# Second FFN of a decoder layer: gate and up products side by side, two of eight row-block pairs by Strassen's seven products, and middle activations turned through a scratch in device memory

## The chip, the cores and the metric

One core of a Trainium2 chip runs the whole kernel. The metric is device time in microseconds (us) of one execution. The kernel before takes 2143.4 us, the median of three runs (2143.32 to 2143.5).

## What is computed

A decoder layer of model width 2048 on 16 learned positions and 256 tokens, in float32. It has a first FFN, a mixing part (sparse attention and a gated convolution, merged and projected by `W_out`) and a second FFN. The change is in the second FFN and the few steps ahead of it:

```python
u = rms_norm(h, ffn2_norm_g[l])
h = h + 0.5 * swiglu(u, ffn2_w_gate[l], ffn2_w_up[l], ffn2_w_down[l])
...
def swiglu(x, w_gate, w_up, w_down):
    return (jax.nn.silu(x @ w_gate) * (x @ w_up)) @ w_down
```

`w_gate` and `w_up` are 2048 x 5632, `w_down` is 5632 x 2048. Only the 256 tokens go through the second FFN.

## The kernel before

Every number is held as two parts, a high one (rounded to the form that TensorE multiplies, float32r) and a low one (what is left). A product is three matmuls: high x high, high x low, low x high.

**The stream.** All weights come in one fixed order through the class `Stream`. A *load* is 1 MB, 128 partitions x 2048 columns, by a DMA from the SP queue (L100) into one of three buffers `raw`. A load is cut into *pieces* of 1024 columns. `split` (L106 to L122) turns a piece into `whi` by ScalarE (L115, a copy with rounding) and `wlo` by VectorE (L116, a difference); there are four buffers of each. `next()` (L137 to L147) gives TensorE the next piece: it first has the piece three ahead split, then runs what is due, and then hands over the piece. So the program order of ScalarE and VectorE is: split of piece n + 3, the work due at step n, split of piece n + 4, and so on. A later load is issued on SP when the last piece of the load three before it has been split.

**Work due.** `later(fn, lag)` puts `fn` behind the split of the step that is `lag - 1` ahead. All of VectorE's and ScalarE's work in the second FFN besides splits is ordered by these lags alone.

**The second FFN** (`ffn_tokens`, L487 to L541) goes through 5632 middle columns in 11 *blocks* of 512, in two groups of 6 and 5. In a block the 256 tokens are two tiles of 128 (j = 1, 2). The activations `act` are stationary, the weights move, 512 columns at a time. Gate first: 16 row blocks of 128 (k), in 8 pieces of two, 12 matmuls a piece (2 tiles x 2 row blocks x 3), into two PSUM banks `pg`. Then up in the same way into `pu`. `gate` (L505) is Silu on ScalarE, `times` (L509) multiplies on VectorE into `s`. As the down products need the middle activations with the middle columns on partitions, `turn_columns` turns `s` into `mt` by 16 transposes of VectorE on 32 partitions each, and `split_into` (L339) makes the two parts in `mid`. After a group's blocks the down products run over `mid`, 512 output columns at a time, and are added to the residual `ht`.

**Ahead of it** the products with `W_out` run in four groups g of 512 columns. `add_out` adds them to `ht` (L1047) and squares on ScalarE; `turn_columns` turns `ht`, and `to_act` (ScalarE L1061, VectorE L1062) makes the activations of row blocks 4g to 4g + 3. For g = 3 the turning runs two quarters a step, inside the first block of the second FFN.

PSUM has eight banks: a ring of four single ones (`mm_tile`) and one of two doubles (`aux_tile`).

Of the kernel before, what the change touches and what calls it, by code (L numbers as in the profile page):

```python
# [9 lines left out]
F32 = mybir.dt.float32  # L10
F32R = mybir.dt.float32r
# [4 lines left out]
P = 128  # L16
# [46 lines left out]
LATER = LINE - META  # L63
SUB = 1024
RAW = 2048


class Stream:
# [7 lines left out]
    def __init__(self, nc, raw_pool, split_pool):  # L76
        self.nc, self.raw_pool, self.split_pool = nc, raw_pool, split_pool
        self.loads, self.subs = [], []
        self.raw, self.ready = {}, {}
        self.n_loaded = self.n_split = self.at = 0  # L80
        self.blocks, self.waiting, self.steps = [], [], []
        self.first = []

    def add(self, src, n, width, cuts=()):
# [21 lines left out]
    def split(self, upto):  # L106
        nc = self.nc
        while self.n_split < min(upto, len(self.subs)):
            g, c, kk, width = self.subs[self.n_split]
            self.load(g + RAW_BUFS)  # L110
            n = kk * width
            raw = self.raw[g][:, c : c + n]
            hi = self.split_pool.tile([P, SUB], F32R, name="whi")
            lo = self.split_pool.tile([P, SUB], F32R, name="wlo")
            nc.scalar.activation(hi[:, :n], raw, AF.Copy)  # L115
            nc.vector.tensor_sub(lo[:, :n], raw, hi[:, :n].bitcast(F32))  # L116
# [45 lines left out]
def tile_decoder_layer(  # L162
# [51 lines left out]
    for n in GROUPS:  # L214
        chunks(wgu2, gu, gu + 8 * n, 512)
        chunks(wd2, down, down + 4 * n, 512)
        gu, down = gu + 8 * n, down + 4 * n
# [90 lines left out]
    def tokens(ps_of, x, n):  # L308

        k = 0  # L310
        while k < n:
            blocks = [st.next()] + st.rest()
            for j, ps in ps_of.items():
                for i, (whi, wlo) in enumerate(blocks):
# [3 lines left out]
                    nc.tensor.matmul(ps, xlo, whi, start=False, stop=k + i == n - 1)  # L318
            k += len(blocks)

    def act_tokens(k, j, part):
# [165 lines left out]
    def ffn_tokens():  # L487

        with tc.tile_pool(name="ffn2", bufs=1, reuse_waits="tile") as fp:
            mid = fp.tile([P, 4 * GROUPS[0], 2, SEQ], F32R, name="mid")  # L490

            late["junk"] = lambda: fp.tile([P, 512], F32, name="junk")
            late["mt"] = lambda: fp.tile([P, 4, SEQ], F32, name="mt", bufs=2)
# [6 lines left out]

            st.later(add_up, 4)
            st.later(root, 5)
            st.later(inverse, 6)

            def gate(pg, s):  # L505
                for j in (1, 2):
                    nc.scalar.activation(s[:, j - 1], pg[j], AF.Silu, scale=rcol[:, 0, j - 1 : j])

            def times(pu, s):  # L509
                for j in (1, 2):  # L510
                    nc.vector.scalar_tensor_tensor(
                        s[:, j - 1], pu[j], rcol[:, 0, j - 1 : j], s[:, j - 1], op0=ALU.mult, op1=ALU.mult
                    )

            def add(d, j, pd, last):
# [6 lines left out]
            for c, n in enumerate(GROUPS):  # L522
                for f in range(n):
                    s = fp.tile([P, 2, 512], F32, name="s", bufs=2)
                    mt = fp.tile([P, 4, SEQ], F32, name="mt", bufs=2)
                    pg = {j: mm_tile(f"pg{j}") for j in (1, 2)}
                    tokens(pg, act_tokens, KD)
                    st.later(lambda pg=pg, s=s: gate(pg, s))
                    pu = {j: mm_tile(f"pu{j}") for j in (1, 2)}
                    tokens(pu, act_tokens, KD)  # L530
                    st.later(lambda pu=pu, s=s: times(pu, s))
# [32 lines left out]
    with ExitStack() as mix:  # L564
# [501 lines left out]
        for g in range(4):  # L1066
# [78 lines left out]
def _layout(x, meta_tokens, ffn1_norm_g, ffn1_w_gate, ffn1_w_up, ffn1_w_down, mix_norm_g, w_in, q_norm_g,  # L1145
# [31 lines left out]
    a["wo"] = _chunks(_tiles(w_out[0], 512))  # L1177
    gu = np.stack([_tiles(ffn2_w_gate[0], 512), _tiles(ffn2_w_up[0], 512)], 1)
    a["wgu2"] = _chunks(gu.reshape(-1, P, KD * 512))
    a["wd2"] = _down_columns(ffn2_w_down[0])  # L1180
# [20 lines left out]
```

## Time and profile before

| what | us |
|---|---|
| median of three runs | 2143.4 |
| span of the profiled execution (first to last instruction) | 2141.4 |
| second FFN, from its first weight load into TensorE to the span's end | 722.6 |
| TensorE busy | 2136.3 |
| TensorE's weight loads busy | 1921.2 |
| VectorE busy | 1325.8 |
| ScalarE busy | 954.5 |

The profiled execution's own time is its span and what lies around it; the median of the runs is 2.0 us above this span. PE is TensorE, PEld its loading of stationary data, DVE is VectorE, ACT is ScalarE, SP the engine whose queue issues the transfers. Lines of groups read: line, engine, operation, tile written <- tiles read, shape, count | busy us, mean ns of one | idle us before it, and what ended most of it. The lines of stretches read: stretch, its length, busy us of PE, PEld, DVE, ACT and POOL with the number of instructions in brackets, granted clock of TensorE, share of DMA time, GB/s. Matmuls are pipelined and their recorded durations overlap.

### The profile page before, as it was taken

To read this page: it belongs to the slowest core of one execution; us is meant where nothing else is said; L and a number is where in the kernel's file an instruction comes from. 1 tells how busy PE (TensorE), PEld (TensorE's weight loads), DVE (VectorE), ACT (ScalarE), POOL (GpSimd) and SP (SyncE) were. 2 spreads that over 40 slices of the span, in tenths; PEclk is the share of its full clock that TensorE was granted. 3 is DMA by queue.
4 is the path that set the end of the run, shared out by engine and by line. 5 is a ranking of instruction groups with operands and counts; after the bars stand their busy time and mean duration, and the time that the engine had idled before them with its cause. 6 is when DMAs were issued, how large, how long until landed. Compare 5 with 4: busy or idle time off the path is not lost.

```text
span 2141.4 us, 30929 instructions
## 1 busy us (share of the span) xinstructions
PE 2136.3 (100%) x12902; PEld 1921.2 (90%) x12902; DVE 1325.8 (62%) x1776; ACT 954.5 (45%) x1173; POOL 10.0 (0%) x28
## 2 busy tenths in 40 slices
PE   9999999999999999999999999999999999999999
PEld 9999999999999998799988888888888888888887
DVE  7555544455555556677686487886676644666664
ACT  6444433344444445565444444454444433444442
POOL 0000000000000000000000000000000000000000
PEclk9999999999999999999999999999999999999999
DMA  7555545555544545454555555555555555555554
GB/s 267 189 181 179 179 180 178 178 177 177 177 178 178 177 170 177 159 176 158 172 188 194 194 189 204 177 183 210 196 196 186 196 191 195 196 197 195 189 200 143
DMA packets 56909, 397.58 MB, mean 186 GB/s; under 512 B 6337, under 2 KB 7105, under 8 KB 9409
## 3 DMA queue, kind: packets, MB, share of 16 engines
q1 hardware_dynamic: 55872, 393.51, 53.4%
q8 instruction: 101, 1.65, 0.3%
q10 hardware_dynamic: 576, 1.05, 0.1%
q0 software_dynamic: 320, 1.05, 0.1%
q14 instruction: 40, 0.32, 0.0%
HBM read 393.49 MB, written 2.10 MB: 185 GB/s over the span
## 4 chain that ended last, share of the span: by engine, by line
PE 99%; DMA 0%; DVE 0%; SPq 0%; ACT 0%; issue 0%; ACTq 0%
PE pd L290 4%; PE pd L289 4%; PE pd L288 4%; PE pu L289 4%; PE pg L289 4%; PE pg L288 4%; PE pu L288 4%; PE pu L290 4%; PE pg L290 4%; PE pg L317 4%; PE pg L318 4%; PE pd L318 4%; PE pu L317 4%; PE pg L316 4%; PE pu L316 4%; PE pd L316 4%
## 5 line engine op out<-in xcount | busy, mean ns | idle before, releaser
L116 DVE TENSOR_TENSOR wlo<-raw,whi 128x1024 fp32r<-128x1024 f32 (+1 forms) x749 | 912.7, 1220 | 780.6 <-ACT whi L115 777.6
L115 ACT ACTIVATE whi<-raw 128x1024 fp32r<-128x1024 f32 (+1 forms) x749 | 788.3, 1055 | 1079.2 <-PE pd L289 146.3
L288 PE MATMUL pd<-mid,whi 128*128 128x272 f32 x704 | 201.7, 286 | 0.0
L289 PE MATMUL pd<-mid,whi 128*128 128x272 f32 x704 | 201.7, 286 | 0.0
L290 PE MATMUL pd<-mid,wlo 128*128 128x272 f32 x704 | 201.7, 286 | 0.0
L288 PE MATMUL pu<-act,whi 128*128 128x272 f32 x672 | 192.6, 287 | 0.0
L289 PE MATMUL pu<-act,whi 128*128 128x272 f32 x672 | 192.5, 287 | 0.0
L288 PE MATMUL pg<-act,whi 128*128 128x272 f32 x672 | 192.5, 286 | 0.0
L289 PE MATMUL pg<-act,whi 128*128 128x272 f32 x672 | 192.5, 286 | 0.0
L290 PE MATMUL pg<-act,wlo 128*128 128x272 f32 x672 | 192.5, 286 | 0.0
L290 PE MATMUL pu<-act,wlo 128*128 128x272 f32 x672 | 192.5, 286 | 0.0
L317 PE MATMUL pg<-wlo,act 128*128 128x512 f32 x352 | 137.2, 390 | 0.0
L318 PE MATMUL pg<-whi,act 128*128 128x512 f32 x352 | 137.1, 389 | 0.0
L316 PE MATMUL pg<-whi,act 128*128 128x512 f32 x352 | 136.9, 389 | 0.0
L316 PE MATMUL pu<-whi,act 128*128 128x512 f32 x352 | 136.9, 389 | 0.0
L317 PE MATMUL pu<-wlo,act 128*128 128x512 f32 x352 | 136.9, 389 | 0.0
L318 PE MATMUL pu<-whi,act 128*128 128x512 f32 x352 | 136.9, 389 | 0.0
L316 PE MATMUL pd<-whi,mid 128*128 128x512 f32 x352 | 136.9, 389 | 0.0
L317 PE MATMUL pd<-wlo,mid 128*128 128x512 f32 x352 | 136.9, 389 | 0.0
L318 PE MATMUL pd<-whi,mid 128*128 128x512 f32 x352 | 136.9, 389 | 0.0
L288 PEld LDWEIGHTS pd<-mid,whi 128*128 128x128 f32 x704 | 132.6, 188 | 0.0
L289 PEld LDWEIGHTS pd<-mid,whi 128*128 128x128 f32 x704 | 132.6, 188 | 0.0
(248 smaller groups left out, 4014.3 us busy)
## 6 DMA issues: line engine op xcount, KB each, us to landing
raw<-in_wgu_dram SPq DMA_DIRECT2D x174, 1024.0 KB, 4.8
raw<-in_wd_dram SPq DMA_DIRECT2D x88, 1024.0 KB, 4.8
raw<-in_wcv_dram SPq DMA_DIRECT2D x24, 1024.0 KB, 4.8
raw<-in_wgc_dram SPq DMA_DIRECT2D x24, 1024.0 KB, 4.9
raw<-in_wga_dram SPq DMA_DIRECT2D x24, 1024.0 KB, 4.8
raw<-in_wo_dram SPq DMA_DIRECT2D x16, 1024.0 KB, 4.8
raw<-in_wqi_dram SPq DMA_DIRECT2D x8, 1024.0 KB, 4.9
raw<-in_wq_dram SPq DMA_DIRECT2D x8, 1024.0 KB, 4.8
```

The costliest lines, as they stand in the source:

```text
L115: nc.scalar.activation(hi[:, :n], raw, AF.Copy)
L116: nc.vector.tensor_sub(lo[:, :n], raw, hi[:, :n].bitcast(F32))
L288: nc.tensor.matmul(ps, whi, xhi, start=first, stop=False)
L289: nc.tensor.matmul(ps, whi, xlo, start=False, stop=False)
L290: nc.tensor.matmul(ps, wlo, xhi, start=False, stop=last)
L316: nc.tensor.matmul(ps, xhi, whi, start=k + i == 0, stop=False)
L317: nc.tensor.matmul(ps, xhi, wlo, start=False, stop=False)
L318: nc.tensor.matmul(ps, xlo, whi, start=False, stop=k + i == n - 1)
```

## The change

**Order of products.** Gate and up are made together. A load holds, for two row blocks k and k + 1, 512 columns each of gate k, up k, up k + 1, gate k + 1, so a block is 8 loads, or *pairs*. Four banks gather c[j, q]: token tile j, and gate (0) or up (1). An ordinary pair is two pieces of 12 matmuls as before.

**Mixed pairs.** Pairs 2 and 5 (`MIXED`) of a block, in the first block only pair 5, are made by Strassen's scheme for a 2 x 2 by 2 x 2 product: seven products instead of eight. A mixed pair has four pieces, a to d, of 2, 2, 2 and 1 products, that is of 6, 6, 6 and 3 matmuls. The sums of weights are made by VectorE (`part`): two before the split of a, two before that of b. The sums of activations (`combos`) are made once, in the first block, for pair 5 at lag 6 and for pair 2 at lag 9. Three products go straight into the banks c, four into side banks m1, m5, m6, m7.

**Combining.** After the second mixed pair `spread` adds m1, m5, m6, m7 in `u` (a copy by ScalarE, four sums by VectorE). After the block `gather` adds `u` to c (four sums), Silu runs on `s`, `times` multiplies.

**Turning.** `turn_blocks` turns 32 x 32 blocks within all 128 partitions (two transposes of 512 columns). `move_blocks` writes the 512 KB to a scratch `hold` in device memory from SP and reads it back by four DMAs from SP with rows of 1 KB, to the partitions where they belong. `split_blocks` then makes the two parts for each token tile, at lag 9 (lag 6 before).

**Around it.** For g = 3 the turning runs one quarter a step as for the other groups; the sums of squares, the root and its inverse run at lags 8, 9 and 10 instead of 4, 5 and 6.

```diff
-            if self.n_split == len(self.subs) or self.subs[self.n_split][0] > g:
+            if self.n_split == len(self.subs) or self.subs[self.n_split][0] > g or c == "b":
                 self.load(g + 1 + RAW_BUFS)
+    def part(self, raw, name):
+        sub, add = self.nc.vector.tensor_sub, self.nc.vector.tensor_add
+        b11, b12, b22, b21 = (raw[:, i * HALF : (i + 1) * HALF] for i in range(4))
+        t3, t2, t4 = (self.mix[:, i * HALF : (i + 1) * HALF] for i in range(3))
+        if name == "a":
+            sub(t3, b22, b12)
+            sub(b12, b12, b11)
+            return raw[:, 2 * HALF :]
+        if name == "b":
+            add(t2, t3, b11)
+            sub(t4, b21, t2)
+            return raw[:, : 2 * HALF]
+        return self.mix[:, : 2 * HALF] if name == "c" else t4
...
+                plan.append([
+                    [(c[1, 1], s[4], 0), (c[1, 0], of(k + 1, 1), 1)],
+                    [(m[1], of(k, 1), 0), (m[5], s[1], 1)],
+                    [(m[7], s[3], 0), (m[6], s[2], 1)],
+                    [(c[2, 0], of(k + 1, 2), 0)],
+                ])
...
-            st.later(add_up, 4)
-            st.later(root, 5)
-            st.later(inverse, 6)
+            st.later(add_up, 8)
+            st.later(root, 9)
+            st.later(inverse, 10)
...
+            def spread(m):
+                nc.scalar.activation(u[:, 0], m[1], AF.Copy)
+                nc.vector.tensor_add(u[:, 2], m[6], u[:, 0])
+                nc.vector.tensor_add(u[:, 1], m[7], u[:, 2])
+                nc.vector.tensor_add(u[:, 2], m[5], u[:, 2])
+                nc.vector.tensor_add(u[:, 3], m[5], u[:, 1])
+            def gather(c, s):
                 for j in (1, 2):
+                    nc.vector.tensor_add(s[:, j - 1], c[j, 0], u[:, j - 1])
+                for j in (1, 2):
+                    nc.vector.tensor_add(u[:, j + 1], c[j, 1], u[:, j + 1])
+                for j in (1, 2):
+                    nc.scalar.activation(s[:, j - 1], s[:, j - 1], AF.Silu, scale=rcol[:, 0, j - 1 : j])
...
+            def move_blocks(mt, x):
+                hold = hbm.tile([P, 4, 2, P], F32, name="hold")
+                nc.sync.dma_start(hold, x)
+                rows = hold.rearrange("(r f) q j c -> q f r (j c)", r=4)
+                for q in range(4):
+                    nc.sync.dma_start(mt[q * 32 : q * 32 + 32], rows[q])
...
-                    for r in range(4):
-                        st.later(lambda mt=mt, s=s, r=r: turn_columns(mt, s, r), 2 + r)
+                    if f == c == 0:
+                        st.later(lambda: combos(1, MIXED[1]), 6)
+                        st.later(lambda: combos(0, MIXED[0]), 9)
+                    now = {i: mixed[i] for i in MIXED[f == c == 0 :]}
+                    quads(cc, m, act_tokens, now, 8, lambda m=m: st.later(lambda: spread(m)))
+                    st.later(lambda cc=cc, s=s: gather(cc, s))
+                    st.later(lambda s=s: times(s), 2)
+                    st.later(lambda xt=xt, s=s: turn_blocks(xt, s), 3)
+                    st.later(lambda mt=mt, xt=xt: move_blocks(mt, xt), 4)
                     to = mid[:, 4 * f : 4 * f + 4]
-                    st.later(lambda to=to, mt=mt: split_into(to[:, :, 0], to[:, :, 1], mt), 6)
+                    st.later(lambda to=to, mt=mt: split_blocks(to, mt), 9)
...
-            per = 2 if g == 3 else 1
             for r in range(4):
-                st.later(lambda g=g, r=r, box=box: turn_columns(box["m"], ht[g], r), 2 + r // per)
-            st.later(lambda g=g, box=box: to_act(g, box["m"]), 2 + 4 // per)
+                st.later(lambda g=g, r=r, box=box: turn_columns(box["m"], ht[g], r), 2 + r)
+            st.later(lambda g=g, box=box: to_act(g, box["m"]), 6)
```

Three places show how the instructions now stand. A row is line, operation, tile written <- tiles read, shape, and a count where it repeats.

VectorE between a block and the next one, before (from the products of `times` on; `mt` is the turned tile):

```order
L511 SCALAR_TENSOR_TENSOR s<-pu_14368,rcol,s 128x512
L511 SCALAR_TENSOR_TENSOR s<-pu_14369,rcol,s 128x512
L116 TENSOR_TENSOR wlo<-raw,whi 128x1024
L389 STREAM_TRANSPOSE mt<-s 32x2x4x32 x4
L116 TENSOR_TENSOR wlo<-raw,whi 128x1024
```

VectorE there after the change (`one` and `three` are banks of c, L143 to L148 the sums of weights of pair 2, `xt` the turned blocks):

```order
L600 TENSOR_TENSOR s<-three,u 128x512
L600 TENSOR_TENSOR s<-one,u 128x512
L602 TENSOR_TENSOR u<-three,u 128x512
L602 TENSOR_TENSOR u<-two,u 128x512
L143 TENSOR_TENSOR mix<-raw 128x512
L144 TENSOR_TENSOR raw<-raw 128x512
L129 TENSOR_TENSOR wlo<-raw,whi 128x1024
L608 SCALAR_TENSOR_TENSOR s<-u,rcol,s 128x512 x2
L147 TENSOR_TENSOR mix<-mix,raw 128x512
L148 TENSOR_TENSOR mix<-raw,mix 128x512
L129 TENSOR_TENSOR wlo<-raw,whi 128x1024
L614 STREAM_TRANSPOSE xt<-s 128x4x4x32 x2
```

Gather, the sums for pair 2, the products and the turning now stand within three pieces, where the turning was spread over four steps.

ScalarE around the splitting of the middle activations, before:

```order
L507 ACTIVATE s<-pg_14210,rcol 128x512
L507 ACTIVATE s<-pg_14211,rcol 128x512
L115 ACTIVATE whi<-raw 128x1024 x13
L340 ACTIVATE mid<-mt 128x4x256
L115 ACTIVATE whi<-raw 128x1024 x3
```

ScalarE there after the change (`mix` are sums of weights):

```order
L604 ACTIVATE s<-s,rcol 128x512 x2
L128 ACTIVATE whi<-raw 128x1024 x2
L128 ACTIVATE whi<-mix 128x1024
L128 ACTIVATE whi<-mix 128x512
L128 ACTIVATE whi<-raw 128x1024 x4
L408 ACTIVATE mid<-mt 128x4x128 x2
L128 ACTIVATE whi<-raw 128x1024 x2
L128 ACTIVATE whi<-mix 128x1024
```

The split of the middle activations stands eight splits behind Silu, right ahead of the splits of the second mixed pair, and now reads what came back from device memory.

VectorE in the first block, before (from the turning of g = 3 to the root):

```order
L389 STREAM_TRANSPOSE mt<-first 32x2x4x32 x8
L116 TENSOR_TENSOR wlo<-raw,whi 128x1024
L1062 SCALAR_TENSOR_TENSOR act<-mt,small,act 128x256 x4
L498 TENSOR_TENSOR sums<-sums 128x2 x2
L499 TENSOR_TENSOR sums<-sums 128x2
```

VectorE there after the change (`comb` holds the combined activations of one pair):

```order
L1192 SCALAR_TENSOR_TENSOR act<-mt,small,act 128x256 x4
L572 TENSOR_TENSOR u<-act 128x512
L573 TENSOR_TENSOR u<-u 128x128
L574 TENSOR_TENSOR u<-u 128x128
L575 TENSOR_TENSOR u<-u 128x128
L576 TENSOR_TENSOR u<-u 128x128
L409 TENSOR_TENSOR comb<-u,comb 128x4x128
L129 TENSOR_TENSOR wlo<-raw,whi 128x1024
L143 TENSOR_TENSOR mix<-raw 128x512
L144 TENSOR_TENSOR raw<-raw 128x512
```

The sums of activations for pair 5 stand between the last activations and the next split; those for pair 2 stand three steps later in the same way, in front of the split of the mixed pair's third piece.

More of the change, by code (lines that the diff above doesn't have):

```diff
@@ L82, in __init__, with add_mixed @@
         self.first = []
+    def add_mixed(self, src):
+        g = len(self.loads)
+        self.loads.append((src, RAW, ()))
+        self.subs += [(g, part, 0, HALF) for part in "abcd"]
     def add(self, src, n, width, cuts=()):
@@ L111, in split @@
             n = kk * width
-            raw = self.raw[g][:, c : c + n]
+            if n:
+                raw = self.raw[g][:, c : c + n]
+            else:
+                raw = self.part(self.raw[g], c)
+                n = raw.shape[1]
+                kk = n // width
             hi = self.split_pool.tile([P, SUB], F32R, name="whi")
@@ L319, in tokens, with trio, quads, of @@
             k += len(blocks)
+    def trio(ps, x, w, first, last):
+        nc.tensor.matmul(ps, x(0), w[0], start=first, stop=False)
+        nc.tensor.matmul(ps, x(0), w[1], start=False, stop=False)
+        nc.tensor.matmul(ps, x(1), w[0], start=False, stop=last)
+    def quads(c, m, x, mixed, n, after_mixed):
+        def of(k, j):
+            return lambda part: x(k, j, part)
+        plan = []
+        for i in range(n):
+            k = 2 * i
+            if i in mixed:
+                s = [None, *(lambda part, q=q, i=i: mixed[i](q, part) for q in range(4))]
+                plan.append([
[4 more added lines that the diff above has]
+                ])
+            else:
+                plan.append([
+                    [(c[j, q], of(k + u, j), q ^ u) for j in (1, 2) for q in ((0, 1), (1, 0))[u]] for u in range(2)
+                ])
+        flat = [id(p[0]) for steps in plan for unit in steps for p in unit]
+        at = 0
+        for i, units in enumerate(plan):
+            for unit in units:
+                blocks = [st.next()] + st.rest()
+                for ps, xx, b in unit:
+                    trio(ps, xx, blocks[b], id(ps) not in flat[:at], id(ps) not in flat[at + 1 :])
+                    at += 1
+            if i == max(mixed):
+                after_mixed()
     def act_tokens(k, j, part):
@@ L487, in ffn_tokens, with combos @@
     def ffn_tokens():
[L489 removed]
+        with ExitStack() as pools:
+            fp = pools.enter_context(tc.tile_pool(name="ffn2", bufs=1, reuse_waits="tile"))
+            hbm = pools.enter_context(tc.tile_pool(name="hold", bufs=2, space=bass.MemoryType.DRAM))
             mid = fp.tile([P, 4 * GROUPS[0], 2, SEQ], F32R, name="mid")
[L492 removed]
+            st.mix = fp.tile([P, 3 * HALF], F32, name="mix")
+            u = fp.tile([P, 4, 512], F32, name="u")
+            comb = fp.tile([P, len(MIXED), 4, 2, P], F32R, name="comb")
+            mixed = {i: lambda q, part, n=n: comb[:, n, q, part] for n, i in enumerate(MIXED)}
+            late["junk"] = lambda: u[:, 0]
+            def combos(n, i):
+                y = u[:, 0].rearrange("p (b j t) -> p b j t", b=2, j=2)
+                z = u[:, 1].rearrange("p (q t) -> p q t", q=4)
+                x = act[:, 2 * i : 2 * i + 2, :, LATER + META :].bitcast(F32).rearrange("p b i (j t) -> p b i j t", j=2)
+                nc.vector.tensor_add(y, x[:, :, 0], x[:, :, 1])
+                nc.vector.tensor_add(z[:, 0], y[:, 0, 1], y[:, 1, 1])
+                nc.vector.tensor_sub(z[:, 1], z[:, 0], y[:, 0, 0])
+                nc.vector.tensor_sub(z[:, 2], y[:, 0, 0], y[:, 0, 1])
+                nc.vector.tensor_sub(z[:, 3], y[:, 1, 0], z[:, 1])
+                split_into(comb[:, n, :, 0], comb[:, n, :, 1], z)
             late["mt"] = lambda: fp.tile([P, 4, SEQ], F32, name="mt", bufs=2)
@@ L515, in add, with split_blocks, banks @@
+            def split_blocks(to, mt):
+                for j in range(2):
+                    x = mt[:, :, j].rearrange("p r (f b) -> p f r b", f=4)
+                    hi, lo = (to[:, :, i, j * P : (j + 1) * P].rearrange("p f (r b) -> p f r b", r=4) for i in range(2))
+                    split_into(hi, lo, x)
+            def banks():
+                one, two, x = mm_tile("one"), mm_tile("two"), aux_tile("three")
+                return [x[:, 0], x[:, 1], one, two]
             def add(d, j, pd, last):
```

41 lines of the change are left out of this document (27 added, 14 removed).

## The prediction

> **What bounds the kernel now.** First the page's span, engine totals and the list of who waited for whom, over the whole run on TensorE and over the second FFN (from 1418.8 us).
>
> ```profile
> span 2141.4 us, 30929 instructions
> PE 2136.3 (100%) x12902; PEld 1921.2 (90%) x12902; DVE 1325.8 (62%) x1776; ACT 954.5 (45%) x1173; POOL 10.0 (0%) x28
> ```
>
> ```profile
> PE start L290 <- DVE wlo L116: 0.2, 1, 0.2
> ```
>
> ```profile
> PEld pg L317 <- DVE wlo L116: 0.6, 2, 0.3
> ```
>
> TensorE never stops: its waits in the second FFN come to 0.6 us. So time falls with matmuls, as long as nothing new makes TensorE wait. What one matmul is worth is read from a stretch, not from its duration, because matmuls overlap:
>
> ```profile
> 1500.00:1600.00 100.00, 100.00 (x443) 82.80 (x442) 66.01 (x80) 43.15 (x43) 0.00 (x0) 1.00 0.58 197
> ```
>
> 442 weight loads in 100 us are 0.226 us a matmul at granted clock 1.00. VectorE is busy for 66 of these 100 us. A block of gate and up is 192 matmuls, 43.4 us. Now the groups of VectorE and ScalarE in that stretch:
>
> ```profile
> L116 DVE TENSOR_TENSOR wlo<-raw,whi 128x1024 fp32r<-128x1024 f32 x39 | 47.8, 1226 | 35.0 <-ACT whi L115 34.7
> L389 DVE STREAM_TRANSPOSE mt<-s 32x256 f32<-32x256 f32 x41 | 17.9, 435 | 0.7
> L511 DVE SCALAR_TENSOR_TENSOR s<-pu,rcol,s 128x512 f32<-128x512 f32 x6 | 4.2, 744 | 0.0
> L341 DVE TENSOR_TENSOR mid<-mt,mid 128x1024 fp32r<-128x1024 f32 x2 | 2.4, 1218 | 0.0
> ```
>
> ```profile
> L115 ACT ACTIVATE whi<-raw 128x1024 fp32r<-128x1024 f32 x39 | 41.3, 1060 | 57.8 <-PE pu L318 29.1 <-PE pg L318 26.6 <-issue 2.2
> L507 ACT ACTIVATE s<-pg,rcol 128x512 f32<-128x512 f32 x4 | 2.5, 675 | 0.0
> ```
>
> whi waits for TensorE: with four buffers, a piece of weights is split when TensorE has left the piece four before it. A split takes 1.06 + 1.23 us and is wanted three pieces (8.1 us) after it may start, so VectorE may run some 5.8 us late before TensorE feels it. That cushion is what the change spends.
>
> **TensorE: what goes.** A mixed pair has 21 matmuls instead of 24. Ten blocks have two mixed pairs and the first has one: 21 x 3 = 63 matmuls, the same 63 by which the order of the instructions is shorter. 63 x 0.226 = **14.2 us** off the path. A block with two takes 186 x 0.226 = 42.0 us.
>
> **VectorE: what comes.** Rows for its new work, from the groups of the later half of the run (512 columns from PSUM, 512 and 256 from SBUF, 2 columns):
>
> ```profile
> L1047 DVE TENSOR_TENSOR first<-po,first 128x512 f32<-128x512 f32 x8 | 5.1, 683 | 0.0
> ...
> L341 DVE TENSOR_TENSOR ms<-mt,ms 128x512 fp32r<-128x512 f32 x2 | 1.3, 686 | 0.0
> L960 DVE TENSOR_TENSOR cy<-t,cy 128x256 f32<-128x256 f32 x2 | 0.9, 426 | 0.2
> ...
> L498 DVE TENSOR_TENSOR sums<-sums 128x2 f32<-128x2 f32 x2 | 0.2, 158 | 0.0
> ```
>
> Before, a block is 16 x 1.23 + 16 x 0.435 + 2 x 0.74 + 1.22 = 29.3 us of 43.4. After: 18 whole splits (22.1) and 2 half ones (1.4), 8 sums of weights, 4 in spread, 4 in gather (16 x 0.68 = 10.9), 2 products (1.5), 2 transposes, 2 halves of the middle (1.4). The trace has a transpose of 256 columns on 32 partitions only, 0.435 us, as much as the 256-column sum (0.426). 512 columns on 128 partitions are then between 0.68 (by columns, like the sum) and 3.5 us (by 32x32 blocks, 64 for 8). I take 0.70, since one block of 32 columns costs no more than 32 columns of a sum. Together 38.7 of 42.0 us, 92%. It fits as a mean; so it must be followed in order. [...]
>
> **The turn from block to block.** Time 0 is the new block's first matmul. Rows for the waits between engines and for a load's transfer:
>
> ```profile
> 1536.27 0.39 PE L318 MATMUL pu<-whi,act 128*128 128x512 f32 x1
> ...
> 1536.33 5.77 SPq L100 DMA_DIRECT2D raw<-in_wgu_dram  x2
> 1536.50 0.39 PE L316 MATMUL pu<-whi,act 128*128 128x512 f32 x1
> ...
> 1536.70 1.06 ACT L115 ACTIVATE whi<-raw 128x1024 fp32r<-128x1024 f32 x1 [1.66 <-PE pu L318]
> ...
> 1537.80 1.23 DVE L116 TENSOR_TENSOR wlo<-raw,whi 128x1024 fp32r<-128x1024 f32 x1 [1.49 <-ACT whi L115]
> ```
>
> whi starts 0.20 us after a piece ends, wlo at 1.3. From 1.3 on VectorE has no pause: 3 splits, 4 sums of gather, 4 of weights, 2 products, 2 transposes. Back to back they follow 0.08 us sooner than their durations: 3 x 1.15 + 8 x 0.62 + 1.36 + 1.4 = 11.2, so the turned tile is ready at 12.5. Then SP writes it out (512 KB) and reads it back in four transfers, which wait for the write's landing. Just ahead, at 11.1 (the turn takes 1.4), SP has issued a weight load. What such a load does (0.25 us windows; last columns DMA share, GB/s), and other transfers:
>
> ```profile
> 1537.75:1538.00 0.25, 0.25 (x3) 0.21 (x2) 0.20 (x1) 0.01 (x1) 0.00 (x0) 1.00 0.18 33
> 1538.00:1538.25 0.25, 0.25 (x3) 0.21 (x2) 0.25 (x1) 0.00 (x0) 0.00 (x0) 1.00 0.92 295
> ...
> 1540.25:1540.50 0.25, 0.25 (x3) 0.21 (x2) 0.00 (x0) 0.23 (x1) 0.00 (x0) 1.00 0.63 262
> 1540.50:1540.75 0.25, 0.25 (x3) 0.21 (x2) 0.24 (x1) 0.00 (x0) 0.00 (x0) 1.00 0.02 0
> ```
>
> ```profile
> DMA to landing us min/median/max: 4.7/4.9/5.1
> ```
>
> ```profile
> raw<-in_wkw_dram SPq DMA_DIRECT2D x1, 640.0 KB, 3.7
> ```
>
> ```profile
> out_dram<-first SPq DMA_DIRECT2D x1, 256.0 KB, 2.1
> ```
>
> ```profile
> 48.52 0.42 SPq L258 DMA_DIRECT2D small<-in_small_dram  x1
> 48.99 0.43 SPq L259 DMA_DIRECT2D ident<-in_ident_dram  x1
> ...
> 50.15 0.43 SPq L261 DMA_DIRECT2D cbias<-in_cbias_dram  x1
> ```
>
> ```profile
> cbias<-in_cbias_dram SPq DMA_DIRECT2D x1, 208.0 KB, 4.3
> ```
>
> Issued at 1536.33, a load moves bytes until about 1540.6, 4.3 us on, at some 390 GB/s; it lands 0.6 later. The 11.1 load moves until 15.4; 512 KB more at 390 GB/s take 1.35, and 0.5 to land: written at 17.2. (256 KB out, alone, land in 2.1; alone 512 KB would take 2.8, so the load costs 1.9.) The reads go out 0.47 apart, the last at 18.7; 128 KB land in 3.7 less 512 KB at 390 GB/s, 2.4 us: back at 21.1, **8.6 us after the turn**. Bounds: 6.7 if the load is not in the way (2.8 + 0.1 + 3.8); 10.6 if the four reads take as long as the four tables, which come to 512 KB too, right behind a load (48.52 until 50.15 + 4.3: 5.9). I stay near the lower part, since nothing is issued ahead of the reads but the write that has landed.
>
> When must it be back? In the ninth step ScalarE and VectorE split it, and both stand in order ahead of the splits of the second mixed pair. After landing: 0.7 ScalarE, 1.3 the two halves on VectorE, then two sums and a split (2.45) and two sums and a split (2.5) for that pair's second piece, 7.1 us with the small gaps. TensorE wants this piece after 4 + 4 pieces of 2.71, four of 1.36, and one of 0.68, that is at 27.8 (its second matmul, which uses wlo, at 28.1). So the tile must be back by 21.0. It is 0.1 to 0.2 late: say 0.2 us of waiting, in the nine blocks that another block follows, **1.8 us**. Each us more of the round trip is 9 us of time; below 8.4 nothing is left to win.
>
> **The first block.** VectorE there has g=3's turning and the combinations of activations. Rows:
>
> ```profile
> L316 PEld LDWEIGHTS pg<-whi,act x352: 187/188/189, 1418.8 to 2006.2; 128*128 128x128 f32 x176
> ```
>
> ```profile
> 1399.77 1.28 DVE L1047 TENSOR_TENSOR first<-po,first 128x512 f32<-128x512 f32 x2
> ...
> 1416.28 1.67 DVE L1062 SCALAR_TENSOR_TENSOR act<-mt,small,act 128x256 fp32r<-128x256 f32 x4
> ...
> 1421.53 1.28 DVE L1047 TENSOR_TENSOR first<-po,first 128x512 f32<-128x512 f32 x2
> ```
>
> L1047 comes 2.7 after the block's start, and in the slower form that g=3 now takes too its activations end 18.2 later: 20.9. One set of combinations is 0.68 + 4 sums of 128 columns (between 0.16 and 0.43; 0.29) + ScalarE's 0.63 and 0.69, about 3.0: 23.9. Split 9 at 25.0, TensorE wants it at 24.7: 0.4 of waiting. Two sums and split 10 (2.45), the sums of squares (0.6), two sums and split 11 (2.45): 30.5 against 29.1, 1.4 more. The root (0.2), the other set (2.9), split 12: 34.7 against 31.7, 3 more, then 0.6: 5.5, less the 0.6 that is there now: **5.0 us**. Bounds 3.5 to 6.5 from the small sums.
>
> **The last block** of the second group has only 8 pieces before its own columns are used, and its split is queued behind piece 11's: 21.7 + 0.2 + 1.06, then ScalarE's first half (0.6) and VectorE's (0.7) while TensorE waits: **2.7 us** (2 to 3.5). In the first group there are ten pieces, and nothing waits.
>
> **At no cost.** The banks now change every three matmuls; so they do in the first FFN's start tiles:
>
> ```profile
> 8.23 0.28 PE L290 MATMUL start<-act,wlo 128*128 128x272 f32 x1
> ...
> 8.60 0.29 PE L290 MATMUL start<-act,wlo 128*128 128x272 f32 x1
> ```
>
> 0.123 us for 272 columns is the rate of 0.226 for 512. ScalarE has 18 x 1.06 + 2 x 0.63 for splits, 1.4 for Silu, 0.6 for spread and 1.3 for the middle, 23.6 of 42.0 us. The norm's root may come four pieces later, since gather scales only at the block's end; that g=3 is turned more slowly is harmless to TensorE, which now uses its columns after 14 pieces instead of 6 (VectorE's delay by it is in the first block's sum). PSUM: spread and gather empty their four banks 2 to 4 pieces before reuse; nothing there. Loads: SP stands behind the write until 17.2, the next load is due at about 16 and wanted near 27; 6 us of cover.
>
> **Sum** against the profiled span: 2141.4 - 14.2 + 5.0 + 2.7 + 1.8 = 2136.7. The median is 2.0 above that span, so 2138.7 us. (Measurement tells 0.2%, 4.3 us.)
>
> **Rivals.** *The round trip eats the gain* (no change, 0.30): back 8.7 to 9.6 us after the turn is 0.3 to 1.2 of waiting in nine blocks, 2139 to 2147.7. For it: small rows (1 KB) into 32 partitions at a time may move slower than the 8 KB rows of a load, and a write may land later behind a load than alone; 0.3 us in all suffices. [...] *The round trip decides* (slower, 0.24): beyond 9.6, at 10.5, the wait is 2 us a block: 9 x 2 - 14.2 + 7.7 = 11.5, 2155. Against it: no transfer behind a single load has 512 KB alone to move that long. *Transposes by blocks* (slower, 0.04): 2 x 2.8 us more before the write, 5.6 x 9: near 2190. That the matmuls do not go is excluded by the count.
>
> **Numbers.** My forecast has 0.42, from 2134.5 (no wait at the turn, the first block at 3.5, the last at 2) to 2139. The upper end, 2153, is a round trip of 10.2; beyond it and below is about 0.2. Faster 0.42, same 0.30, slower 0.28.
>
> **What would show it.** Right: 12,839 matmuls; TensorE waits once per block at L354 to L356 on wlo of the second mixed pair for under 0.3 us, 5 us in the first block around 1445, 2.7 near 2050; mt lands 8.6 us after L614 ends. Wrong: reads that land after 9.6, transposes above 1 us, or TensorE waiting at the first mixed pair's c.

## The result and the profile after

| what | before | after |
|---|---|---|
| median of the runs, us | 2143.4 | 2156.1 (4 runs, 2155.1 to 2156.6) |
| span of the profiled execution, us | 2141.4 | 2154.8 |
| matmuls | 12,902 | 12,839 |
| VectorE busy, us | 1325.8 | 1404.9 |

The change makes the kernel slower: 1.0059 times the time before, with a 95% interval of 1.0045 to 1.0073. The forecast was 2138.7 and its range ended at 2153.0, so both were wrong. The span grew by 13.4 us although the 63 matmuls went.

First the page of the changed kernel, its span and engine totals:

```profile
span 2154.8 us, 31085 instructions
PE 2130.8 (99%) x12839; PEld 1910.0 (89%) x12839; DVE 1404.9 (65%) x1859; ACT 994.2 (46%) x1239; POOL 10.0 (0%) x28
```

TensorE's busy time fell by 5.5 us only, because a recorded matmul that stands behind a pause is longer (0.50 and 0.51 us instead of 0.39 at the two waits shown below); the weight loads (PEld) show the pauses better. The list of who waited for whom, in the second FFN (from 1420 us), says where they are:

```profile
ACT mid L408 <- DMA mt<-hold: 52.8, 9, 6.9
DVE mid L409 <- ACT mid L408: 45.7, 9, 6.1
PEld three L355 <- DVE wlo L129: 22.6, 20, 2.0
...
PEld two L354 <- ACT whi L128: 2.3, 1, 2.3
PEld pd L348 <- ACT mid L408: 2.1, 1, 2.1
...
PEld two L355 <- DVE wlo L129: 1.1, 1, 1.1
PEld pd L350 <- DVE mid L409: 1.0, 1, 1.0
```

Nine times, once for each turn from a block to another one, ScalarE stands 5.4 to 6.9 us at the splitting of the middle activations (L408) until the reads from the scratch land, VectorE stands behind it (L409), and TensorE then waits for the low part of a piece of weights. Of the 20 waits at L355 for `wlo` of a product in bank three, 18 belong to these turns and two to the first block. The two waits at `pd` are the last block of the second group.

The same stretch of 100 us as before:

```profile
1500.00:1600.00 100.00, 97.03 (x424) 79.02 (x424) 81.77 (x96) 52.10 (x57) 0.00 (x0) 1.00 0.64 221
```

There are 424 weight loads instead of 442: 18 times 0.226, 4.1 us of this stretch are lost, at a granted clock of 1.00. It holds two turns, so a turn costs about 2 us.

Now one turn step by step. The block's first matmul begins at 1512.78 us. VectorE from the turning of the products on (columns: start, duration, engine, line, tiles, shape, count, in brackets the idle time ahead and what ended it):

```profile
1523.86 1.30 DVE L614 STREAM_TRANSPOSE xt<-s 128x512 f32<-128x512 f32 x2
...
1536.71 1.29 DVE L409 TENSOR_TENSOR mid<-mt,mid 128x512 fp32r<-128x512 f32 x2 [5.30 <-ACT mid L408]
1537.92 0.68 DVE L143 TENSOR_TENSOR mix<-raw 128x512 f32<-128x512 f32 x1
1538.63 0.69 DVE L144 TENSOR_TENSOR raw<-raw 128x512 f32<-128x512 f32 x1
1539.24 1.22 DVE L129 TENSOR_TENSOR wlo<-raw,whi 128x1024 fp32r<-128x1024 f32 x1
1540.38 0.68 DVE L147 TENSOR_TENSOR mix<-mix,raw 128x512 f32<-128x512 f32 x1
1541.10 0.69 DVE L148 TENSOR_TENSOR mix<-raw,mix 128x512 f32<-128x512 f32 x1
1541.71 1.22 DVE L129 TENSOR_TENSOR wlo<-raw,whi 128x1024 fp32r<-128x1024 f32 x1
```

SP's queue, and ScalarE's split, in the same stretch:

```profile
1525.19 0.33 SPq L621 DMA_DIRECT2D hold<-xt  x1
1531.24 1.75 SPq L624 DMA_DIRECT2D mt<-hold  x4
```

```profile
1536.04 1.16 ACT L408 ACTIVATE mid<-mt 128x512 fp32r<-128x512 f32 x2 [6.09 <-DMA mt<-hold]
```

TensorE's weight loads at the second mixed pair, where it waits:

```profile
1539.08 0.19 PEld L354 LDWEIGHTS three<-whi,comb 128*128 128x128 f32 x1
1540.52 0.19 PEld L355 LDWEIGHTS three<-wlo,comb 128*128 128x128 f32 x1 [1.25 <-DVE wlo L129]
...
1542.98 0.19 PEld L355 LDWEIGHTS three<-wlo,act 128*128 128x128 f32 x1 [1.24 <-DVE wlo L129]
```

The turned tile is ready at 1525.16, 12.4 us into the block. The write is issued at once, and the reads, which wait for its landing, go out at 1531.24: the write took 6.05 us. The tile is back when ScalarE starts, at 1536.04, 4.80 later, 10.85 after the write's issue and 23.3 into the block. From there the chain runs as foreseen: the low part of the mixed pair's first piece is ready 4.4 us after the tile, that of its second piece 6.9 (1541.71 + 1.22). TensorE stands for both, 1.25 and 1.24 us.

This turn is one of nine. From the write's issue to ScalarE's start the trips take 10.2 to 11.6 us, 10.6 in the mean (6.0 for the write, 4.6 for the reads), and TensorE's waits behind one trip come to 1.8 to 3.3 us, in each case the trip less some 8.4.

The page's rows of the transfers for the whole run (count, size, median us from issue to landing):

```profile
hold<-xt SPq DMA_DIRECT2D x11, 512.0 KB, 5.9
mt<-hold SPq DMA_DIRECT2D x44, 128.0 KB, 2.8
```

### The profile page after: what moved, and what is told of

It reads as the page before. It is cut to its first block, busy times and chain, and to the rows that moved or that the text cites. A ratio compares the mean times of both kernels' runs of the same rounds, so it can differ in the third digit from the quotient of the medians.

```text
span 2154.8 us, 31085 instructions
## 1 busy us (share of the span) xinstructions
PE 2130.8 (99%) x12839; PEld 1910.0 (89%) x12839; DVE 1404.9 (65%) x1859; ACT 994.2 (46%) x1239; POOL 10.0 (0%) x28
## 5 line engine op out<-in xcount | busy, mean ns | idle before, releaser
L322 PEld LDWEIGHTS pd<-mid,wlo 128*128 128x128 f32 x704 | 132.7, 188 | 0.0
L355 PE MATMUL three<-wlo,act 128*128 128x512 f32 x310 | 121.9, 393 | 8.5 <-DVE wlo L129 8.5
L320 PEld LDWEIGHTS pg<-act,whi 128*128 128x128 f32 x672 | 126.6, 188 | 0.0
L321 PEld LDWEIGHTS pu<-act,whi 128*128 128x128 f32 x672 | 126.6, 188 | 0.0
L320 PEld LDWEIGHTS pu<-act,whi 128*128 128x128 f32 x672 | 126.6, 188 | 0.0
L321 PEld LDWEIGHTS pg<-act,whi 128*128 128x128 f32 x672 | 126.6, 188 | 0.0
```

What stands on the lines that cost most here:

```text
L320: nc.tensor.matmul(ps, whi, xhi, start=first, stop=False)
L321: nc.tensor.matmul(ps, whi, xlo, start=False, stop=False)
L322: nc.tensor.matmul(ps, wlo, xhi, start=False, stop=last)
L355: nc.tensor.matmul(ps, x(0), w[1], start=False, stop=False)
```

## The experiments

Two theories stood at the start. **Round trip:** the tile comes back too late for the place at which ScalarE and VectorE split it, and this makes nearly all of the loss. **VectorE:** its new sums and transposes fill it (82 of 100 us above), and TensorE would wait with any round trip.

### e1_no_trip: the middle activations split without the trip

The blocks are split as they were turned, without the write and the reads. The kernel so leaves out the move to the partitions where they belong.

```diff
-                    st.later(lambda mt=mt, xt=xt: move_blocks(mt, xt), 4)
-                    st.later(lambda to=to, mt=mt: split_blocks(to, mt), 9)
+                    st.later(lambda to=to, xt=xt: split_blocks(to, xt), 9)
```

> The trip through device memory is left out: the middle activations are split straight from the turned blocks (so the down products use wrongly placed middle columns). Theory (the tile that comes back late, 10.9 us after the turn, holds up ScalarE and VectorE in front of the second mixed pair): the waits at the second mixed pair, 20.5 us over nine blocks, go; the 5.6 us of the first block and the 3.1 us of the last stay. About 2136 us. Rival (VectorE has too much to do in a block, 38.7 of 42 us, so that it is late with or without the trip): most of the 20.5 us stays, 2150 us or more.

Measured: 2138.8 us, 0.9982 of before (0.9972 to 0.9991), span 2136.1. All 18 waits at the turns are gone; the first and the last block wait as before. The stretch of 100 us in this kernel:

```profile
1500.00:1600.00 100.00, 100.00 (x443) 82.81 (x442) 84.87 (x100) 53.73 (x60) 0.00 (x0) 1.00 0.57 204
```

VectorE is busier than in the changed kernel, 84.87 us, and TensorE has its 442 weight loads. So VectorE's share alone makes nothing late, and the round trip costs 2154.8 - 2136.1 = 18.7 us, 2.1 a turn. (Between the medians it is 17.3; the runs of this kernel spread over 3.6 us, which the last section takes up.)

### e2_load_behind: the next load of weights goes out behind the trip

A mixed pair's second piece is the last one cut from its load (c and d come from the sums). The change issues the next load right there, and it stands on SP ahead of the write. Here it goes out when the whole pair has been split.

```diff
-            if self.n_split == len(self.subs) or self.subs[self.n_split][0] > g or c == "b":
+            if self.n_split == len(self.subs) or self.subs[self.n_split][0] > g:
```

> The weight load that now goes out after piece b of a mixed pair goes out after piece d, as for other loads, so it stands behind the write and the reads of the scratch instead of ahead of them. Theory (the write took 6.0 us because the load's bytes were ahead of it): the write lands in about 3 us, the tile is back some 3 us sooner, 7.9 us after the turn, and no block waits at the second mixed pair: 2136 to 2138 us. Rival (write and reads are slow by themselves, 1 KB rows and device memory): the write stays near 5 us, the waits go down by half at most, 2146 us or more. A second rival: the load itself now comes too late, with waits on raw.

Measured: 2141.1 us, 0.9988 (0.9979 to 0.9998), span 2139.5. The write's row on the page, and SP's queue at the same turn:

```profile
hold<-xt SPq DMA_DIRECT2D x11, 512.0 KB, 2.6
```

```profile
1524.31 0.33 SPq L621 DMA_DIRECT2D hold<-xt  x1
1526.94 1.75 SPq L624 DMA_DIRECT2D mt<-hold  x4
1528.79 2.24 SPq L108 DMA_DIRECT2D raw<-in_wgu_dram  x3
```

```profile
1532.73 1.16 ACT L408 ACTIVATE mid<-mt 128x512 fp32r<-128x512 f32 x2 [3.65 <-DMA mt<-hold]
```

The write alone lands in 2.6 us instead of 5.9. ScalarE's split begins at 1532.73, so this trip is 8.4 us (the reads take 5.8, with three loads issued right behind them), and TensorE doesn't wait behind it, as the prediction's limit of 8.4 has it. It is the longest of the nine; the others take 6.8 to 7.7. The waits at the turns are 0.7 us in all, three of 0.19 to 0.30, and the trip isn't their cause: they stand behind trips of 6.9 to 7.7 us, and ahead of each ScalarE waits 1.9 to 2.6 us for a load of weights. So the second rival, that the load itself now comes late, holds in small. The time is some 3 us above the expected 2136 to 2138; the next run's stretches show where.

### e3_split_later: the tile may come back later

The trip stays as it is; its split stands behind the second mixed pair.

```diff
-                    st.later(lambda to=to, mt=mt: split_blocks(to, mt), 9)
+                    st.later(lambda to=to, mt=mt: split_blocks(to, mt), 9 if f == n - 1 else 15)
```

> The split of the middle activations goes from lag 9 to lag 15, behind the second mixed pair, in all blocks but the last of a group. The trip, its bytes and its place on SP stay as they are. Theory (only the place in order matters): no wait at the second mixed pair, 2136 us, with the trip still 10 to 11 us. Rival (the traffic of the trip or VectorE's total work costs the time): no gain of more than a few us, 2150 us.

Measured: 2140.7 us, 0.9986 (0.9977 to 0.9995), span 2139.7. The write still lands after 6.0 us, and no turn makes TensorE wait. So it isn't the length of the trip by itself but the place of the split in two queues that run in order. The expected time was 2136 us: this run and e2_load_behind end some 3.5 us behind e1_no_trip in their spans. The stretches of the first and the last block show why; first e1_no_trip, then e3_split_later:

```profile
1440.00:1460.00 20.00, 16.04 (x61) 11.92 (x60) 17.71 (x34) 11.63 (x14) 0.00 (x0) 0.91 0.35 117
...
2040.00:2060.00 20.00, 17.73 (x78) 14.04 (x77) 9.75 (x10) 8.24 (x9) 1.25 (x2) 1.00 0.59 190
```

```profile
1440.00:1460.00 20.00, 16.30 (x57) 11.98 (x56) 17.66 (x36) 11.35 (x14) 0.00 (x0) 0.84 0.35 112
...
2040.00:2060.00 20.00, 17.73 (x70) 13.87 (x69) 9.75 (x10) 6.61 (x9) 1.25 (x2) 0.91 0.62 220
```

The waits are the same in both; the granted clock is not, 0.84 for 0.91 and 0.91 for 1.00: 20 x 0.07 + 20 x 0.09 = 3.2 us. In e2_load_behind it is 0.83 and 0.91. The last section comes back to it.

### e4_no_mixed: the trip with ordinary pairs

All pairs are ordinary, with all their matmuls, and spread, the sums of gather and the combinations are left out; the turning, the trip and the place of the split stay. Its core:

```diff
-            if i % 8 in MIXED[i < 8 :]:
+            if False:
...
-                    now = {i: mixed[i] for i in MIXED[f == c == 0 :]}
+                    now = {}
```

> No mixed pairs: gate and up side by side and the trip through device memory alone, all eight products everywhere, no sums of weights or activations, no spread and gather. Theory (the trip is hidden as long as the pieces ahead are whole ones): nothing waits between blocks, only the last block waits for its split, 2 to 3 us: 2145 to 2147 us. Rival (the trip costs its 20 us by itself): 2160 us.

Measured: 2146.0 us, 1.0014 (1.0005 to 1.0023), span 2144.2. The write lands in 5.9 us here too, yet no turn waits; only the last block's two waits at `pd` are left (2.09 and 1.04), and they account for the 2.8 us over before's span. The same trip is covered where the next pieces are whole ones of 12 matmuls with one split each: a lag counts pieces, and with whole ones ScalarE comes to the split 13.2 to 13.7 us after the write's issue, when the tile has long landed. In the changed kernel, where four of the pieces between are the short ones of a mixed pair, it stands there at 1536.04 - 6.09 = 1529.95, 4.8 us after the write's issue, and the quick pieces of the second mixed pair follow, the first two with two sums each besides the split.

### e5_comb_later and e7_first_plain: the first block

In the first, the sums of activations for pair 2 come five steps later; in the second, the first block has no mixed pair at all (24 matmuls where the change has 21), and both sets of sums come at lags 11 and 13.

```diff
-                        st.later(lambda: combos(0, MIXED[0]), 9)
+                        st.later(lambda: combos(0, MIXED[0]), 14)
```

```diff
-                        st.later(lambda: combos(1, MIXED[1]), 6)
-                        st.later(lambda: combos(0, MIXED[0]), 9)
-                    now = {i: mixed[i] for i in MIXED[f == c == 0 :]}
+                        st.later(lambda: combos(1, MIXED[1]), 11)
+                        st.later(lambda: combos(0, MIXED[0]), 13)
+                    now = {} if f == c == 0 else mixed
```

> In the first block the second set of activation sums goes from lag 9 to lag 14, behind the split of the mixed pair's last piece. All else as in the change. Theory (VectorE's queue in front of piece c makes the wait there): of the first block's four waits (0.86, 1.31, 2.34, 1.07 us) the last two go, 3.3 us; the half clock that follows them for 3.4 us or more, 1.7 us, should go too, if it comes from the waits: 2151 to 2153 us. Rival (the half clock has another cause): 2153 us with the granted clock still at 0.5 for a few us.

Measured: 2152.3 us, 1.0042 (1.0028 to 1.0055), span 2149.9. The pause of 2.34 us shrinks to 0.28, but the 1.07 us behind it stays, against what was expected, two new ones of 0.25 and 0.60 follow in the first block, and the second block has one of 0.61. The granted clock is 1.00 here, so 1.7 of the 4.9 us that the span gains are clock. Moved work isn't gone in a stretch where VectorE is 17 us busy of 20.

> The first block has no mixed pair (three matmuls more, 0.7 us); both sets of activation sums go to lags 11 and 13. All else as in the change. Theory: all 5.6 us of waits of the first block go, and the half clock there: 2156.1 - 5.2 - 1.7 + 0.7 = 2150 us, the waits between blocks as they were. Rival (the first block's VectorE work only moves, and TensorE waits a few pieces later): 2154 us or more.

Measured: 2148.5 us, 1.0024 (1.0015 to 1.0034), span 2146.5. The first block's waits are gone altogether, for the price of three matmuls, and the granted clock is 1.00 there; of the turns' 18 waits 17 stay.

### e9_last_early: the last block too

As e3_split_later, and in the last block of a group the turning and the trip start earlier and the split stands two steps nearer.

```diff
-                    st.later(lambda xt=xt, s=s: turn_blocks(xt, s), 3)
-                    st.later(lambda mt=mt, xt=xt: move_blocks(mt, xt), 4)
+                    end = f == n - 1
+                    st.later(lambda xt=xt, s=s: turn_blocks(xt, s), 2 if end else 3)
+                    st.later(lambda mt=mt, xt=xt: move_blocks(mt, xt), 2 if end else 4)
...
-                    st.later(lambda to=to, mt=mt: split_blocks(to, mt), 9)
+                    st.later(lambda to=to, mt=mt: split_blocks(to, mt), 7 if end else 15)
```

> Split of the middle activations at lag 15 in the inner blocks; in the last block of a group the turning and the trip go to lag 2, ahead of a weight load, and the split to lag 7. Theory: no wait at the second mixed pair and none in the last block; only the first block's 5.6 us and its half clock stay: 2141.4 - 14.2 + 5.2 + 1.7 + 2 = 2136 us. Rival (the last block's wait comes back because the tile is not there yet): as with lag 15 alone, 2139 to 2141 us.

Measured: 2136.4 us, 0.9967 (0.9955 to 0.9979), span 2134.7. The two waits at `pd` are gone, and only the first block's are left.

### e8_best: both repairs together

This is e7_first_plain with the edits of e9_last_early.

> Plain first block, split at lag 15 in inner blocks, early turning in the last block of a group: nothing left that makes TensorE wait, 20 mixed pairs. Theory: 60 matmuls less than before, 13.6 us, and nothing given back, granted clock 1.000: 2129 to 2130 us. Rival (VectorE at 92% in a mixed block cannot keep up even when nothing is late): 2135 us or more.

Measured: 2129.9 us, 0.9936 (0.9923 to 0.9948), span 2128.2. TensorE waits for no other engine from 1420 us on, and the stretches that paused are full:

```profile
1440.00:1460.00 20.00, 20.00 (x90) 16.53 (x90) 15.85 (x32) 11.07 (x13) 0.00 (x0) 1.00 0.60 211
1500.00:1600.00 100.00, 100.00 (x443) 82.81 (x442) 85.81 (x102) 52.83 (x58) 0.00 (x0) 1.00 0.62 220
2040.00:2060.00 20.00, 20.00 (x90) 16.54 (x89) 9.78 (x9) 8.16 (x8) 1.25 (x2) 1.00 0.71 237
```

It has 60 matmuls fewer than before; 60 x 0.226 = 13.6 us, and its span is 13.2 below before's. Nearly the whole worth of the matmuls is kept, with the inner blocks' writes behind a load as slow as they were (5.9 to 6.7 us). This version beats both kernels.

### e10_wide_read: small rows on the write's side

The write goes out as four transfers with the 1 KB rows, so that one read of 512 KB has rows of 4 KB into all 128 partitions. All else is as in the change.

```diff
-                nc.sync.dma_start(hold, x)
-                rows = hold.rearrange("(r f) q j c -> q f r (j c)", r=4)
-                for q in range(4):
-                    nc.sync.dma_start(mt[q * 32 : q * 32 + 32], rows[q])
+                rows = hold.rearrange("(q f) r j c -> r f q (j c)", q=4)
+                for r in range(4):
+                    nc.sync.dma_start(rows[r], x[r * 32 : r * 32 + 32])
+                nc.sync.dma_start(mt, hold)
```

> The rearranging goes to the write: four writes to the scratch with rows of 1 KB out of 32 partitions each, then one read of 512 KB with 4 KB rows into 128 partitions. The change else. In the change the four reads took 4.8 us from the first issue to the last landing, with bytes at some 220 GB/s, where loads move at 390. Theory (rows of 1 KB into 32 partitions move slowly): the one read moves at the loads' rate and lands in 3.5 us or a little more, the writes take 7 us or more, and the trip as a whole is about as long: 2150 to 2156 us. Rival (the next load, which goes out right behind the reads, slows them): the read still takes about 5 us, and the time is above 2156 us.

Measured: 2145.9 us, 1.0012 (1.0003 to 1.0021), span 2143.4. SP's queue at the same turn:

```profile
1523.42 2.05 SPq L623 DMA_DIRECT2D hold<-xt  x4
1529.51 0.34 SPq L624 DMA_DIRECT2D mt<-hold  x1
```

```profile
1532.82 1.16 ACT L408 ACTIVATE mid<-mt 128x512 fp32r<-128x512 f32 x2 [4.63 <-DMA mt<-hold]
```

The write takes 6.1 us from the first issue as before, the read 3.3 instead of 4.8, the trip 9.4. The read came out as the theory had it; the writes did not, 6.1 us where 7 or more were expected, and so the time lies below both theories'. The trip is 1.45 us shorter, the span 11.4. From 2040 to 2060 this run has a granted clock of 0.91 as e3_split_later has, 20 x 0.09 = 1.8 us that the changed kernel doesn't lose; without it the gain is 13.2, where nine times 1.45 are 13.1: one share for each of the nine turns. The edit changes two things at once, though, the rows and the number of transfers. To issue four reads takes SP 1.75 us, to issue one 0.34; the difference of 1.41 is about the whole gain. So which of the two made the read quicker isn't shown.

### e11_three: three mixed pairs in a block

e8_best with pairs 1, 3 and 6 mixed and one buffer less for `mt`.

```diff
-MIXED = (2, 5)
+MIXED = (1, 3, 6)
...
+                        st.later(lambda: combos(2, MIXED[2]), 15)
```

> The version without waits with three mixed pairs of eight (1, 3 and 6) instead of two in all blocks but the first; one buffer for the tile that comes back instead of two. Ten blocks lose three more matmuls each, 6.8 us. VectorE was busy 36 us of a 42 us block; a third pair adds 1.5 splits and four sums, about 4.2 us, to 40 of 41.4 us. Theory (a block's work still fits, but its order leaves no reserve): TensorE waits about 1 us a block, 2130 to 2136 us, no gain over two pairs. Rival (the pieces between give the reserve back): 2123 us, a further gain.

Measured: 2152.9 us, 1.0051 (1.0034 to 1.0068), span 2149.3, a miss. The stretch, and TensorE's waits in one block:

```profile
1500.00:1600.00 100.00, 95.57 (x412) 76.31 (x411) 91.52 (x110) 53.21 (x60) 0.00 (x0) 1.00 0.58 210
```

```profile
1560.41 0.19 PEld L355 LDWEIGHTS two<-wlo,comb 128*128 128x128 f32 x1 [0.76 <-DVE wlo L129]
1562.34 0.19 PEld L355 LDWEIGHTS one<-wlo,act 128*128 128x128 f32 x1 [0.68 <-DVE wlo L129]
1564.65 0.19 PEld L355 LDWEIGHTS three<-wlo,act 128*128 128x128 f32 x1 [1.79 <-DVE wlo L129]
```

VectorE is at 92 of 100 us, not at its end, but gather, products and turning now fall between the pieces of a mixed pair, and TensorE waits 3.2 us for split pieces at such a turn (the three rows), and in most blocks 0.56 more for a bank that `spread` has yet to read. The trip isn't late here: the write lands in 2.6 us, and the split stands some 18 us behind its issue. So with three pairs the waits are VectorE's, as the second theory had it; with two they aren't. Whether another order of its work would remove them wasn't tried.

## Why the prediction was wrong, point by point

**The step that failed is the size of the round trip.** The prediction took "8.6 us after the turn" and stayed "near the lower part" of 6.7 to 10.6; it is 10.85 in the turn shown and 10.6 in the mean of the nine (10.2 to 11.6), at that upper bound and beyond it. The range of times ended at a trip of 10.2, which is the shortest that came. Both halves were short. The write was to land 4.7 us after its issue and took 6.05. These are the bytes of the load and the write together, in the changed kernel:

```profile
1526.00:1528.00 2.00, 2.00 (x11) 1.65 (x10) 2.00 (x4) 1.46 (x3) 0.00 (x0) 1.00 1.13 352
1528.00:1530.00 2.00, 2.00 (x10) 1.66 (x9) 2.00 (x3) 1.95 (x2) 0.00 (x0) 1.00 0.78 309
1530.00:1532.00 2.00, 2.00 (x10) 1.68 (x9) 1.41 (x2) 0.00 (x0) 0.00 (x0) 1.00 0.11 39
1532.00:1534.00 2.00, 2.00 (x10) 1.65 (x10) 0.00 (x0) 0.00 (x0) 0.00 (x0) 1.00 0.61 176
```

The prediction let both move at a lone load's 390 GB/s; they move at 309 to 352. The reads were to be back after 3.9 us and took 4.8: from 1532 to 1534, a stretch that holds their start and nothing of the write, 176 GB/s moved, not 390. Its reason, that "nothing is issued ahead of the reads but the write that has landed", was true and did not help, since the reads are slow by their own form, four issues with small rows (e10_wide_read: 3.3 us as one read with wide rows).

**What a late tile costs was right.** "Each us more of the round trip is 9 us of time; below 8.4 nothing is left to win": e10_wide_read took 1.45 us off the trip and 13.2 off the span, the half clock left out, and behind the trip of 8.4 us in e2_load_behind nothing waits. Turn by turn it fits too: in the changed kernel the wait is the trip less 8.4 us, in e10_wide_read (trips of 8.9 to 9.8 us, waits of 0.4 to 1.2) the trip less 8.5, each within 0.1. By this rule the mean of 10.6 is some 2.2 us a turn, and e1_no_trip shows 2.1: 18.7 us in place of 1.8. So the rival "the round trip decides", with 2155 us for a trip of 10.5, is what happened. It had 0.24, and what it lacked was the price, not the mechanism. The argument brought against it, that no transfer behind a single load moves so long, was an argument from loads alone.

The prediction saw one short wait a turn; the trace has two, because once the first piece of the pair is late the second, which takes TensorE less long than its sums and split take VectorE, adds about 1.24 each time.

**The matmuls** went as counted, 12,839 are left, and e8_best shows their worth: 13.2 us of span for 60.

**The turning before the trip** was right: two transposes in 1.30 us (0.70 each was forecast), the tile ready at 12.4 (12.5).

**The first block** was right in size and place: in the stretch from 1440 to 1460 the changed kernel has 60 weight loads where before has 89, 6.6 us. A half clock behind the pauses is 1.7 of it (the last section), so the waits cost 4.9, against 5.0. Its four waits of 0.4, 1.4, 3 and 0.6 us (5.4 in all, where it has 5.5) are 0.86, 1.31, 2.34 and 1.07 in the trace. Of the half clock the prediction has no term; with it the block lies at its upper bound of 6.5.

**The last block** was right: 2.09 + 1.04 us of waiting. In e1_no_trip, which waits there just as long, the row from 2040 to 2060 above has 77 weight loads for 89 in e8_best, 12 x 0.226 = 2.7 us, against 2.7.

**What was put at no cost** (PSUM, ScalarE, the root, the loads) shows no wait of TensorE. e4_no_mixed shows the new turning of g = 3 harmless as well.

The sum by the measured terms is 2141.4 - 14.2 + 18.7 + 6.6 + 2.7 = 2155.2, against 2154.8. Of the 18.1 us between the forecast span of 2136.7 and this one, the round trip has 16.9.

## What to carry to other kernels

Where a step waits for a transfer in a queue that runs in order, count not only how long the transfer takes but how early behind it the next needed piece stands: trips of 10.2 to 11.6 us cost 18.7 us in all ahead of a mixed pair, and with the split six steps later (e3_split_later) no turn waited. A trip through device memory that no row shows should be taken at its upper bound or beyond, and the program built so that this doesn't matter: moving a split by six steps made nothing wait here. And before a new scheme is given up or praised, look at its first and last round, where its set-up and its end have no cover: here they took 9.3 of the 14.2 us.

## What the runs showed of the hardware

**Clock behind short pauses.** The waits of the first block in the changed kernel, and the stretches around them:

```profile
1453.33 0.19 PEld L354 LDWEIGHTS two<-whi,comb 128*128 128x128 f32 x1 [2.34 <-ACT whi L128]
1454.59 0.29 PEld L355 LDWEIGHTS two<-wlo,comb 128*128 128x128 f32 x1 [1.07 <-DVE wlo L129]
```

```profile
1454.00:1456.00 2.00, 1.41 (x3) 1.16 (x4) 1.86 (x8) 1.69 (x2) 0.00 (x0) 0.61 0.02 8
1456.00:1458.00 2.00, 2.00 (x6) 1.57 (x5) 2.00 (x3) 0.87 (x1) 0.00 (x0) 0.53 0.00 0
```

Two pauses of 2.34 and 1.07 us stand here with one weight load between them. From within the second one on, the clock is granted at half for 3.41 us (1454.45 to 1457.86), which costs 2 x 0.39 + 2 x 0.47 = 1.7. In e2_load_behind and e3_split_later it lasts about twice as long (granted clock 0.83 and 0.84 from 1440 to 1460), and there it also follows the last block's 2.09 + 1.04 (0.91 from 2040 to 2060), which in e1_no_trip it doesn't (1.00; the rows above). The turns' pauses of 1.25 and 1.24 us, which lie 2.5 us apart, cost no clock (1.00 from 1500 to 1600), and e5_comb_later, with 0.28 and 1.07, none (1.00 from 1440 to 1460). How these pauses lie can be read from stretches of 3.41 us, the length of the half clock in the changed kernel. Here they are in e2_load_behind, laid so that one begins where the clock falls:

```profile
1449.90:1453.31 3.41, 1.52 (x6) 0.68 (x4) 2.39 (x7) 2.12 (x4) 0.00 (x0) 1.00 0.80 291
1453.31:1456.72 3.41, 2.65 (x7) 2.15 (x7) 3.27 (x9) 1.98 (x3) 0.00 (x0) 0.50 0.04 17
1456.72:1460.14 3.42, 3.42 (x9) 2.64 (x8) 3.37 (x4) 2.50 (x3) 0.00 (x0) 0.50 0.42 101
2043.82:2047.23 3.41, 1.14 (x5) 0.31 (x3) 1.92 (x4) 2.10 (x3) 0.00 (x0) 1.00 0.98 406
2047.23:2050.64 3.41, 3.41 (x8) 2.74 (x9) 0.54 (x1) 0.00 (x0) 0.00 (x0) 0.50 0.92 320
```

The clock is at half for two whole stretches and, 2047.23 - 1453.31 = 593.92 = 174 x 3.4133 us later, for one more. In the changed kernel it falls once more at the program's end, at 2154.18, which is 696.32 = 204 x 3.4133 us behind 1457.86. So the changes measured in these two traces lie whole numbers of 3.413 us apart. Laid out so from 1420 us on, the changed kernel has these three stretches, the first and the last ahead of its falls, the other one, at a turn, the least busy that no fall follows:

```profile
1451.04:1454.45 3.41, 0.88 (x3) 0.19 (x1) 2.46 (x5) 2.75 (x4) 0.00 (x0) 1.00 0.72 293
2021.06:2024.48 3.42, 1.66 (x6) 1.05 (x6) 3.39 (x5) 2.29 (x3) 0.00 (x0) 1.00 0.33 137
2150.77:2154.18 3.41, 0.28 (x2) 0.00 (x0) 0.69 (x1) 0.00 (x0) 0.00 (x0) 1.00 0.40 154
```

TensorE was busy (the first figure behind the length) for 0.88 and 0.28 us ahead of these falls, for 1.52 and 1.14 ahead of the two in e2_load_behind shown above, and for 1.66 at the turn, where the clock stayed at 1.00. That the sum of the pauses within one such stretch decides, and so the place of the same pauses among the stretches, is an estimate from these five; more is not shown. No single pause ahead of the first block's fall in the changed kernel was longer than 2.34 us. The executions of e1_no_trip, which has the pauses of the first and the last block, spread over 3.6 us (2137.5 to 2141.1), those of e8_best, which has none, over 0.8 (2129.2 to 2130.0).

**A write behind a load.** 512 KB to device memory landed in 2.6 us in e2_load_behind, where the write goes out ahead of the load, and in 5.9 in the changed kernel, right behind a load of 1 MB on the same queue (medians of 11 writes each).

**Four reads or one.** At the turn shown, the changed kernel's four reads of 128 KB in rows of 1 KB into 32 partitions each took 4.8 us from the first issue to the last landing; in e10_wide_read one read of the same 512 KB with rows of 4 KB into 128 partitions took 3.3. Most of the difference can be the issue on SP, 1.75 us against 0.34; the share of the small rows isn't shown. The four small writes of e10_wide_read took no longer than the one large one, behind the load that both had ahead of them.
